# One 512-column product in place of two of 256 in the z gate of the second mixer

## The chip, the cores and the metric

The kernel runs on one core of a Trainium2 chip. The metric is device time in microseconds (us) of one execution. Before the change three runs took 1121.48, 1123.04 and 1123.1 us; the median is 1123.04 us. Lower is better.

## The reference

The program is a two-layer language-model block on 256 tokens with a width of 2048, all in float32. Layer one is an RWKV-7 mixer, layer two a sparse attention (NSA) mixer with 16 heads of 128 columns, each on a normalised input and with a residual. The part that the change touches is the gate z of the second mixer. Cut to what matters:

```python
def nsa_mixer(u, shared, w_in, gate_b, w_o):
    proj = u @ w_in                      # u: 256 tokens x 2048
    q  = rope_partial(proj[..., :2048])  # 16 heads
    gl = proj[..., 2048:2096] + gate_b   # 48 branch gates
    z  = proj[..., 2096:]                # 2048 columns: the z gate
    o  = attention(q, gl, shared)        # 256 x 2048
    o  = o * silu(z)
    return o @ w_o
```

`u` is the hidden state times the inverse root-mean-square of its token and a gain per column. The kernel multiplies by the gain before the product and by the token's factor after it.

## The kernel before

**Split numbers.** The matrix products take operands of the type float32r. Each float32 operand is split into a high part (the value copied into float32r, on ACT) and a low part (what is left, a subtraction on DVE, in some cases on POOL). A product of two operands is then three matrix products: high by high, high by low, low by high. The program calls the parts of a weight `whi` and `wlo`, those of a token tile `mh` and `ml`.

**Weights.** All weight matrices stream from HBM once, in 128x1024 pieces on the queue of SP (`Weights.load`, buffers `wraw`, five of them). A piece is split into units of 128x512 by `Weights.ensure`: line 206 is the ACT copy into `whi`, line 191 the subtraction into `wlo`. Five buffers of each exist in this stage, and a unit is taken by `W.get()`.

**Token tiles.** A mixed or normalised input is held transposed, as 16 tiles of 128 columns by 256 tokens (index k), each with a high and a low buffer. Two rings of 16 buffers serve all phases (`ring`, line 409): ring 0 holds the inputs v, k, y and ob, ring 1 holds w, a, z, r and u. `u`, the input of the second mixer, is written by `turn_h` (lines 1397 and 1398) long before it is read.

**Two forms of the product.** `rows_step` (lines 608, 609 and 611) has the tokens as the stationary operand and 512 (or 384, 432 or 256) weight columns as the moving one. `cols_step` (lines 626 to 628) has a 128x128 block of the weight as the stationary operand and 256 tokens as the moving one; its result is transposed, with columns on partitions. The z gate of the second mixer uses `cols_block`, which is four calls of `cols_step`: for each of 16 k three products of 256 columns, in the order `whi` by `mh`, `whi` by `ml`, `wlo` by `mh`, all added up in one half of a PSUM bank.

**The attention stage.** Twenty-one phases run one after the other in the order of the list `QZ` (line 80): five `phase_q`, which project the queries with `rows_step` (432, 512 or 384 columns), and 16 `phase_z`, one for each head. The list is `(0, 25, 24, 1, 2, 23, 22, 21, 3, 20, ...)`, where numbers below 10 are q and n stands for the gate of head n - 10 otherwise. Beside them a background generator, `attn_all`, computes the attention of the heads in pairs, last heads first. Its instructions have a higher rank (`atPE=1000`), and the program's scheduler, which simulates the engines in time, puts all of them into one fixed order for each engine. So the matrix products of the attention stand between those of the phases.

After its 48 products `phase_z` multiplies the sum by `RST`, the tokens' factors (line 1597, DVE, from PSUM), takes the hyperbolic tangent on ACT (line 1599) and combines both on DVE (line 1600): z times (tanh(z/2) + 1). When a pair of heads has its attention result `og` (line 1717, ACT, one buffer) and both gates, `flush` multiplies them on POOL (line 1731), splits the product (lines 1733 and 1734) and hands it to the output projection as `ob`.

**After the attention.** `phase_bo` is the output projection, with `rows_step`, from k = 15 down in its first block of 512 columns. When the last of the attention is done its buffers are released, and `open_fin` loads the residual into `h` (line 1765, 2 MB) and the final gain. `accumulate` (line 1771) adds the products to `h`. The last lines normalise and store.

**PSUM.** The products of the phases rotate over three banks (`accp("acc")`), the scores, transposes and sums of the attention have five others.

Of the kernel before, what the change touches and what calls it, by code (L numbers as in the profile page):

```python
# [11 lines left out]
F32R = mybir.dt.float32r  # L12
AF = mybir.ActivationFunctionType
OP = mybir.AluOpType
# [3 lines left out]
T, D, NK = 256, 2048, 16  # L18
# [199 lines left out]
def hybrid_kernel(ctx: ExitStack, tc: tile.TileContext, a: dict, out: bass.AP):  # L218
    nc = tc.nc
    V, S, G, PE = nc.vector, nc.scalar, nc.gpsimd, nc.tensor  # L220
# [36 lines left out]
    def accp(name="acc"):  # L257
        n = turn.get(name, 0)
        turn[name] = n + 1
        b = role[name]  # L260
        return psum.tile([128, 512], F32, name=f"bank{b[n % len(b)]}", bufs=1)
# [12 lines left out]
    W = Weights(tc, wpool, RAWB, AHEAD)  # L274
# [67 lines left out]
    mixp = ctx.enter_context(tc.tile_pool(name="mixp", bufs=1))  # L342
# [61 lines left out]

    RINGS = {"v": 0, "k": 0, "y": 0, "ob": 0, "w": 1, "a": 1, "z": 1, "r": 1, "u": 1}
    owners = ([], [])
    used = set()

    def ring(nm, k):
        i = RINGS[nm]  # L410
        h = mixp.tile([128, T], F32R, name=f"mh{i}", bufs=NK)
        l = mixp.tile([128, T], F32R, name=f"ml{i}", bufs=NK)
        owners[i].append((nm, k))
        return h, l

# [4 lines left out]
    def split_into(src, nm, k):  # L420
        h, l = ring(nm, k)
        S.activation(h, src, AF.Copy)  # L422
        V.tensor_tensor(l, src, h.bitcast(F32), op=OP.subtract)
        mixed[(nm, k)] = (h, l)
# [44 lines left out]
    if True:  # L469
# [20 lines left out]
        keep_warm(4)  # L490
        W.hold = True
        h0, l0 = ring("v", 0)
        m0 = ph1.tile([128, T], F32, name="mtmp", bufs=3)

# [100 lines left out]
    N256, N512 = 109.0, 216.0  # L595

    def need(key):
        if key not in mixed:
            sch.require(lambda: key in mixed)
        return mixed[key]  # L600
# [20 lines left out]
    def cols_step(o, nm, q, first=True, **kw):  # L621
        wh, wl = W.get()
        for s in range(4):
            k = 4 * q + s
            mh, ml = need((nm, k))
            PE.matmul(o, wh[:, s, :], mh, start=k == 0 and first, stop=False, **kw)  # L626
            PE.matmul(o, wh[:, s, :], ml, start=False, stop=False, **kw)  # L627
            PE.matmul(o, wl[:, s, :], mh, start=False, stop=k == NK - 1, **kw)  # L628
            yield 3 * N256

    def cols_block(nm, o):
        for q in range(4):
            yield from cols_step(o, nm, q)
# [42 lines left out]
    def phase_z(nb):  # L676
        ps = two()
        yield from rows_block(ps, "z", 512)
        for tt in range(2):
            th = kph.tile([128, 512], F32, name="zth", bufs=2)  # L680
            S.activation(th, ps[tt], AF.Tanh, scale=0.5)
            S.activation(th, th, AF.Copy, scale=0.5, bias=0.5)
            V.tensor_tensor(th, ps[tt], th, op=OP.mult)
            store_heads(zd, nb, tt, th, nc.sync)
# [266 lines left out]
    for nm, i in ZK:  # L951
        sch.run((phase_z3() if i == 3 else phase_z(i)) if nm == "z" else phase_k(i))
# [217 lines left out]
    def turn_y(U):  # L1170
        yt = [PBK[U][:, x * 512:x * 512 + 256] for x in range(2)]
        for i in range(NCH):
            for x, h in each:
                r = H(x, h)
                PE.matmul(yt[x][R[h], i * 64:i * 64 + 64], OU[U][r, x, i, :], ident[r, r], start=True, **mm)
        made = [ring("y", 2 * U + x) for x in range(2)]
        for x, (yh, yl) in enumerate(made):
            S.activation(yh, yt[x], AF.Copy)
            mixed[("y", 2 * U + x)] = (yh, yl)
        for x, (yh, yl) in enumerate(made):  # L1180
            V.tensor_tensor(yl, yt[x], yh.bitcast(F32), op=OP.subtract)
        sch.t += 350
# [367 lines left out]
    RST = at.tile([128, T], F32, name="RST")  # L1550
# [39 lines left out]
            qd[h0 + g] = (qh, ql)  # L1590

    def phase_z(h):
        o = accp("acc")[:, :T]
        yield from cols_block("u", o)
        sch.require(lambda: h + ZB >= HEADS or ("ob", h + ZB) in mixed)
        z = at.tile([128, T], F32, name="zT", bufs=ZB)
        V.tensor_tensor(z, o, RST, op=OP.mult)
        th = at.tile([128, T], F32, name="zth", bufs=2)
        S.activation(th, z, AF.Tanh, scale=0.5)
        V.scalar_tensor_tensor(z, th, 1.0, z, op0=OP.add, op1=OP.mult)  # L1600
        zdone[h] = z
# [147 lines left out]
    for ph in QZ:  # L1749
        sch.run(phase_q(ph) if ph < 10 else phase_z(ph - 10))  # L1750
# [95 lines left out]
```

## Time and profile before

| | us |
|---|---|
| runs | 1121.48, 1123.04, 1123.1 |
| median of the runs | 1123.04 |
| span of the profiled execution, first to last instruction | 1121.7 |
| PE busy | 1101.1 |
| DVE busy | 826.7 |
| ACT busy | 720.8 |
| POOL busy | 332.1 |
| z gates of the second mixer, first to last product | 802.6 to 1024.0 |

The profile is of one execution. Its span runs from the first to the last instruction, and the runs' median is 1.3 us longer than it. A busy PE in this profile is not a PE at its peak, since its instructions overlap: a matrix product is shown with its whole latency, and the next starts before it ends. What tells the speed of PE is the distance between the starts of two products. PEld is the loading of the stationary operand, which overlaps with the products.

### The profile page before, as it was taken

The numbers are of one execution on the slowest core, as the hardware profiler recorded it, in microseconds if no ns is written. First come the engines' busy times: TensorE is split into PE (matmuls) and PEld (weight loads), VectorE is DVE, ScalarE is ACT, GpSimd is POOL, SyncE is SP. The second block draws the span as 40 slices with busy tenths as digits, with TensorE's granted clock in tenths as the row PEclk, the third lists the DMA queues.
The fourth block names the chain that finished last, engine by engine and source line by source line (L and its number), as shares of the span: only waits on it lengthen the run. The fifth ranks groups of instructions, "written<-read, shape, count | busy, mean of one in ns | idle before, by whom it ended". The sixth has DMA issues, their size and how long they took to land.

```text
span 1121.7 us, 25742 instructions
## 1 busy us (share of the span) xinstructions
PE 1101.1 (98%) x9496; PEld 975.5 (87%) x9496; DVE 826.7 (74%) x1765; ACT 720.8 (64%) x1704; POOL 332.1 (30%) x424
## 2 busy tenths in 40 slices
PE   9999999999999989999999999999999999999997
PEld 7788899898888878989888888888989999999886
DVE  6999976679886997666667776764666877766564
ACT  7767777677774456655557766665566777765553
POOL 1300045424338657754100010101323333332012
PEclk9999999999999999999999999999999999999999
DMA  7458878777879989975578667675756355554853
GB/s 258 154 189 247 244 206 257 241 215 225 251 233 264 248 191 231 225 185 148 170 239 276 195 203 258 197 256 155 199 142 163 107 153 132 132 132 163 297 184 109
DMA packets 241775, 226.34 MB, mean 202 GB/s; under 512 B 51536, under 2 KB 193200, under 8 KB 241264
## 3 DMA queue, kind: packets, MB, share of 16 engines
q1 hardware_dynamic: 236320, 219.17, 67.3%
q0 software_dynamic: 4864, 4.92, 1.7%
q8 instruction: 75, 1.23, 0.5%
q10 hardware_dynamic: 464, 0.59, 0.1%
q14 instruction: 52, 0.43, 0.1%
HBM read 200.48 MB, written 24.15 MB: 200 GB/s over the span
## 4 chain that ended last, share of the span: by engine, by line
PE 80%; DVE 10%; DMA 4%; issue 3%; ACT 3%; SPq 0%; POOL 0%; ACTq 0%; DVEq 0%; POOLq 0%
PE bank L609 12%; PE bank L611 12%; PE bank L608 12%; PE bank L626 8%; PE bank L628 7%; PE bank L627 7%; PE bank L234 5%; DVE wlo L191 5%; ACT whi L206 2%; PE pair L611 1%; PE pair L608 1%; PE pair L609 1%; DMA wraw<-in_kv_w_dram 1%; PE bank L1192 1%; PE bank L776 1%
## 5 line engine op out<-in xcount | busy, mean ns | idle before, releaser
L191 DVE TENSOR_TENSOR wlo<-wraw,whi 128x512 fp32r<-128x512 f32 (+2 forms) x616 | 437.9, 724 | 164.9 <-ACT whi L206 161.5
L206 ACT ACTIVATE whi<-wraw 128x512 fp32r<-128x512 f32 (+2 forms) x664 | 403.0, 618 | 193.8 <-PE bank L611 68.0
L626 PE MATMUL bank<-mh,whi 128*128 128x256 f32 (+1 forms) x800 | 234.7, 293 | 0.5 <-ACT whi L206 0.5
L628 PE MATMUL bank<-mh,wlo 128*128 128x256 f32 (+1 forms) x800 | 228.2, 286 | 1.0 <-DVE wlo L191 1.0
L627 PE MATMUL bank<-ml,whi 128*128 128x256 f32 (+1 forms) x800 | 227.5, 284 | 0.0
L609 PE MATMUL bank<-wlo,mh 128*128 128x512 f32 (+3 forms) x576 | 218.1, 379 | 1.3 <-DVE wlo L191 1.2
L611 PE MATMUL bank<-whi,ml 128*128 128x512 f32 (+3 forms) x576 | 215.3, 376 | 0.0
L608 PE MATMUL bank<-whi,mh 128*128 128x512 f32 (+3 forms) x576 | 190.3, 377 | 0.6 <-ACT Vt L1490 0.3
L626 PEld LDWEIGHTS bank<-mh,whi 128*128 128x128 f32 (+1 forms) x800 | 151.4, 189 | 5.9 <-ACT whi L206 1.1
L628 PEld LDWEIGHTS bank<-mh,wlo 128*128 128x128 f32 (+1 forms) x800 | 151.3, 189 | 2.7 <-DVE wlo L191 1.4
L627 PEld LDWEIGHTS bank<-ml,whi 128*128 128x128 f32 (+1 forms) x800 | 151.7, 190 | 1.6
L609 PEld LDWEIGHTS bank<-wlo,mh 128*128 128x128 f32 x576 | 108.3, 188 | 18.6 <-DVE wlo L191 2.7
L611 PEld LDWEIGHTS bank<-whi,ml 128*128 128x128 f32 x576 | 108.3, 188 | 16.1
L608 PEld LDWEIGHTS bank<-whi,mh 128*128 128x128 f32 x576 | 107.0, 188 | 17.1 <-ACT Vt L1490 0.7
L191 POOL TENSOR_TENSOR wlo<-wraw,whi 128x512 fp32r<-128x512 f32 (+2 forms) x48 | 57.4, 1196 | 186.6 <-ACT whi L206 163.5
L609 PE MATMUL bank<-wlo,kvh 128*128 128x512 f32 x192 | 76.1, 396 | 0.0
L611 PE MATMUL bank<-whi,kvl 128*128 128x512 f32 x192 | 75.2, 392 | 0.0
L608 PE MATMUL bank<-whi,kvh 128*128 128x512 f32 x192 | 66.7, 392 | 0.4 <-ACT whi L206 0.4
L422 ACT ACTIVATE mh<-mtmp 128x256 fp32r<-128x256 f32 x95 | 37.7, 409 | 17.9 <-DVE mtmp L429 16.5
L429 DVE SCALAR_TENSOR_TENSOR mtmp<-xx,prm,xn 128x256 f32<-128x256 f32 x95 | 46.5, 501 | 0.1
L609 PEld LDWEIGHTS bank<-wlo,kvh 128*128 128x128 f32 x192 | 36.1, 188 | 7.7 <-issue 0.4
L918 POOL DMA_DIRECT2D Yb<-yvd x60 | 33.2, 558 | 31.5 <-PE pair L1106 25.7
(351 smaller groups left out, 1925.8 us busy)
## 6 DMA issues: line engine op xcount, KB each, us to landing
wraw<-in_a_w_rkvz_dram SPq DMA_DIRECT2D x128, 512.0 KB, 5.4
wraw<-in_kv_w_dram SPq DMA_DIRECT2D x48, 512.0 KB, 4.4
wraw<-in_b_w_in_dram SPq DMA_DIRECT2D x40, 512.0 KB, 4.1
wraw<-in_a_w_o_dram SPq DMA_DIRECT2D x32, 512.0 KB, 4.8
wraw<-in_b_w_o_dram SPq DMA_DIRECT2D x32, 512.0 KB, 4.4
spd<-sp SPq DMA_DIRECT2D x16, 642.0 KB, 5.5
wraw<-in_b_w_in_dram SPq DMA_DIRECT2D x24, 384.0 KB, 3.3
wraw<-in_cmp_w_dram SPq DMA_DIRECT2D x16, 512.0 KB, 4.0
```

The costliest lines, as they stand in the source:

```text
L191: eng.tensor_tensor(lv, src, hv.bitcast(F32), op=OP.subtract)
L206: self.nc.scalar.activation(hv, src, AF.Copy)
L234: return fn(*args, **kw)
L422: S.activation(h, src, AF.Copy)
L429: V.scalar_tensor_tensor(m, xx[:, k, :], mu[:, k:k + 1], xn[:, k, 1:], op0=OP.mult, op1=OP.add)
L608: PE.matmul(o, mh[:, ts], wh[:, 0, :], start=k == ends[0], stop=False)
L609: PE.matmul(o, mh[:, ts], wl[:, 0, :], start=False, stop=False)
L611: PE.matmul(o, ml[:, ts], wh[:, 0, :], start=False, stop=k == ends[1])
L626: PE.matmul(o, wh[:, s, :], mh, start=k == 0 and first, stop=False, **kw)
L627: PE.matmul(o, wh[:, s, :], ml, start=False, stop=False, **kw)
L628: PE.matmul(o, wl[:, s, :], mh, start=False, stop=k == NK - 1, **kw)
L918: eng.dma_start(Yb[U % 2][at:at + 32, x, :, 32 * q:32 * q + 32], inverse(yvd[U // 4], ((2 * U + x) % 8) * 2 + h, q))
```

## The change

Ring 1 gets one buffer of 512 columns for each k instead of two of 256: the high part in the left half, the low part in the right half. In `phase_z` the two products with the stationary operand `whi` become one with 512 moving columns, which writes the whole PSUM bank: left half high by high, right half high by low. The product with `wlo` goes on adding to the left half. At the end ACT copies the right half out of PSUM, DVE adds it to the left half and DVE multiplies by `RST` in a step of its own. Ring 0, the other phases and the order of the phases stay. The other phases that use ring 1 read the halves as before.

```diff
     def ring(nm, k):
         i = RINGS[nm]
-        h = mixp.tile([128, T], F32R, name=f"mh{i}", bufs=NK)
-        l = mixp.tile([128, T], F32R, name=f"ml{i}", bufs=NK)
+        if i:
+            both = mixp.tile([128, 2 * T], F32R, name="mhl", bufs=NK)
+            h, l = both[:, :T], both[:, T:]
+            beside[(nm, k)] = both
+        else:
+            h = mixp.tile([128, T], F32R, name="mh", bufs=NK)
+            l = mixp.tile([128, T], F32R, name="ml", bufs=NK)
         owners[i].append((nm, k))
         return h, l
...
     def phase_z(h):
-        o = accp("acc")[:, :T]
-        yield from cols_block("u", o)
+        o = accp("acc")
+        for q in range(4):
+            wh, wl = W.get()
+            for s in range(4):
+                k = 4 * q + s
+                mh, ml = need(("u", k))
+                PE.matmul(o, wh[:, s, :], beside[("u", k)], start=k == 0, stop=False)
+                PE.matmul(o[:, :T], wl[:, s, :], mh, start=False, stop=k == NK - 1)
+                yield 3 * N256
         sch.require(lambda: h + ZB >= HEADS or ("ob", h + ZB) in mixed)
         z = at.tile([128, T], F32, name="zT", bufs=ZB)
-        V.tensor_tensor(z, o, RST, op=OP.mult)
         th = at.tile([128, T], F32, name="zth", bufs=2)
+        S.activation(th, o[:, T:], AF.Copy)
+        V.tensor_tensor(z, o[:, :T], th, op=OP.add)
+        V.tensor_tensor(z, z, RST, op=OP.mult)
         S.activation(th, z, AF.Tanh, scale=0.5)
         V.scalar_tensor_tensor(z, th, 1.0, z, op0=OP.add, op1=OP.mult)
         zdone[h] = z
```

More of the change, by code (lines that the diff above doesn't have):

```diff
@@ L406, in hybrid_kernel @@
     owners = ([], [])
+    beside = {}
     used = set()
```

## The prediction, made before the change was run

> **What bounds the kernel now.** I read the page first: its busy shares, its clock and its chain of waits.
>
> ```profile
> span 1121.7 us, 25742 instructions
> ...
> PE 1101.1 (98%) x9496; PEld 975.5 (87%) x9496; DVE 826.7 (74%) x1765; ACT 720.8 (64%) x1704; POOL 332.1 (30%) x424
> ...
> PEclk9999999999999999999999999999999999999999
> ...
> PE 80%; DVE 10%; DMA 4%; issue 3%; ACT 3%; SPq 0%; POOL 0%; ACTq 0%; DVEq 0%; POOLq 0%
> ```
>
> PE holds 80% of the chain that ends last. But a share over the whole kernel says nothing about this stage, so next I took the busy time in the stage of the gates, and PE's waits from 790 to 1030 us.
>
> ```profile
> core 0: us, PE busy (x) PEld busy (x) DVE busy (x) ACT busy (x) POOL busy (x), PEclk, DMA share, GB/s
> 802.00:1025.00 223.00, 223.00 (x1561) 212.78 (x1560) 162.54 (x395) 155.30 (x440) 71.41 (x70) 1.00 0.53 142
> ```
>
> ```profile
> PE bank L609 <- DVE wlo L191: 0.4, 1, 0.4
> ```
>
> PE has work in all 223 us, at full clock (1.00), and waited once, for 0.4 us. DVE works 73% of the stage and ACT 70%, DMA 53%. Here PE alone sets the pace, and a shorter stream of products is a shorter stage. Whether a wide product makes it shorter is a question of the distance between starts, which the listing in order of time shows.
>
> **What the product costs.** First a gate as it is: 46 products of 256 columns stand in this listing from the first to the last, 45 steps.
>
> ```profile
> 802.58 0.28 PE L626 MATMUL bank<-mh,whi 128*128 128x256 f32 x1
> 802.70 0.28 PE L627 MATMUL bank<-ml,whi 128*128 128x256 f32 x1
> ...
> 807.97 0.28 PE L626 MATMUL bank<-mh,whi 128*128 128x256 f32 x1
> ```
>
> (807.97 - 802.58) / 45 = 119.8 ns. The 0.28 us of a row is latency, not the price. Then a stretch of products of 512 columns in the output projection, 16 steps.
>
> ```profile
> 1049.83 0.39 PE L608 MATMUL bank<-whi,mh 128*128 128x512 f32 x1
> 1050.05 0.39 PE L609 MATMUL bank<-wlo,mh 128*128 128x512 f32 x1
> ...
> 1053.45 0.39 PE L611 MATMUL bank<-whi,ml 128*128 128x512 f32 x1
> ```
>
> (1053.45 - 1049.83) / 16 = 226.3 ns. So 256 more columns cost 226.3 - 119.8 = 106.5 ns, and what is left of the narrow step, 119.8 - 106.5 = 13.3 ns, is paid once per product whatever its width. Two narrow ones cost 239.6 ns, one wide one 226.3: the change saves this 13.3 ns at each pair. The number of columns that stream through PE, 768 for each k, stays. This is why the saving is small: a third of the products goes, but only a fixed part of each goes with it.
>
> The number of pairs comes from the groups by shape in the stage, one such row for each of the lines 626 to 628:
>
> ```profile
> L628 PE MATMUL bank<-mh,wlo 128*128 128x256 f32 x256 | 73.4, 287 | 0.0
> L627 PE MATMUL bank<-ml,whi 128*128 128x256 f32 x256 | 73.1, 286 | 0.0
> ```
>
> 256 pairs (16 gates by 16 k) by 13.3 ns are **3.4 us less on PE**.
>
> In the new stream wide and narrow products alternate, which neither stretch shows. The nearest rows are places where one of the attention's wide products falls into a gate:
>
> ```profile
> 1020.76 0.28 PE L626 MATMUL bank<-mh,whi 128*128 128x256 f32 x1
> 1020.88 0.39 PE L234 MATMUL bank<-Th,vh 128*128 128x512 f32 x1
> 1021.11 0.28 PE L627 MATMUL bank<-ml,whi 128*128 128x256 f32 x1
> ...
> 1021.70 0.28 PE L626 MATMUL bank<-mh,whi 128*128 128x256 f32 x1
> 1021.82 0.40 PE L234 MATMUL bank<-Tl,vh 128*128 128x512 f32 x1
> 1022.06 0.27 PE L234 MATMUL bank<-cst,P 128*128 128x128 f32 x1
> ```
>
> Narrow to wide is 0.12 us and wide to narrow 0.23 (1020.88 to 1021.11), together 0.35 against three narrow steps of 0.36: some 10 ns saved. With the 0.24 of the second place, ahead of a transpose, it is 0. So the ends are 0 and 3.4 us; I take 3.3, by the first place and the pure stretches, since the second place differs in what follows.
>
> [...]
>
> **What is added.** Each gate gets one copy on ACT from PSUM and one operation on DVE. The nearest rows are an ACT copy of this shape from PSUM (line 1588), and for DVE the operations of the gate itself: 1597 reads PSUM, as the new addition will, and 1600 reads SBUF, as the new multiplication will.
>
> ```profile
> L1588 ACT ACTIVATE qh<-bank x16: 366/385/395, 808.5 to 967.8; 128x256 fp32r<-128x256 f32 x16
> ```
>
> ```profile
> L1597 DVE TENSOR_TENSOR zT<-bank,RST x16: 414/424/425, 809.0 to 1024.3; 128x256 f32<-128x256 f32 x16
> L1599 ACT ACTIVATE zth<-zT x16: 403/413/428, 809.6 to 1025.1; 128x256 f32<-128x256 f32 x16
> L1600 DVE SCALAR_TENSOR_TENSOR zT<-zth,zT x16: 380/420/1374, 810.0 to 1025.8; 128x256 f32<-128x256 f32 x16
> ```
>
> ACT gets 16 x 0.385 = 6.2 us, DVE 16 x 0.42 = 6.7 us. ACT goes from 155.3 to 161.5 of now 219.7 us (74%), DVE from 162.5 to 169.3 (77%). Both stay below PE, so I put them at 0 us. Their cover is the time in which ACT waits for PE, when it has run ahead with the weights:
>
> ```profile
> ACT whi L206 <- PE bank L611: 23.0, 41, 1.0
> ACT whi L206 <- PE bank L627: 16.4, 24, 2.0
> ACT Th L1684 <- PE bank L234: 11.0, 15, 1.9
> ```
>
> The two rows of the weights alone are 39.4 us, six times the 6.2. Without that cover the price would be up to 6.2 + 6.7 = 12.9 us.
>
> The gate also comes later after its last product: by the copy, the second DVE operation and ACT's queue, 0.8 us at least. While the copy stands at the head of ACT's queue for the last product, the splits of weights behind it wait too, and PE waits for those; but line 1597 made DVE stand there in the same way before, and five units of weights are split ahead. Two things use the gate or its bank next. The PSUM bank is needed again after at least one other gate of 48 x 0.12 = 5.8 us, so 0.8 us are free. And the attention's `og` waits on POOL:
>
> ```profile
> POOL og L1731 <- DVE zT L1600: 14.0, 6, 5.5
> ```
>
> ```profile
> 978.51 0.75 POOL L1734 TENSOR_TENSOR ml<-og,mh 128x256 fp32r<-128x256 f32 x1 [0.59 <-ACT mh L1733]
> ```
>
> ```profile
> 982.08 0.60 ACT L1717 ACTIVATE og<-bank 128x512 f32<-128x512 f32 x1 [1.08 <-PE bank L234]
> ```
>
> In 6 of 16 cases the gate is last, but at this one the buffer is free at 979.3 and refilled at 982.1, for which ACT waits on PE: 2.8 us of room. And each earlier gate has brought the stream forward by 0.2 us. I put this at 0, too.
>
> **What is only moved.** With one buffer for both halves a reader of the high part could wait for the writing of the low part, in all phases of ring 1. PE's wait for a freshly written tile is in the view of line 626:
>
> ```profile
>   ACT mh L422: 0.4, 2
> ```
>
> Two waits, 0.4 us in 800 products; waiting for the low half as well would be 0.4 us more each, 0.8 in all. I take 0, as the product that needs the low half comes 0.12 us later anyway. No DMA and no step on SP's or POOL's queue is moved.
>
> **The end of the stage.** The last pair's attention ends on POOL; then the residual is loaded, and DVE adds the first block to it.
>
> ```profile
> 1031.80 2.27 POOL L1734 TENSOR_TENSOR ml<-og,mh 128x256 fp32r<-128x256 f32 x2
> ```
>
> ```profile
> 1034.97 0.46 SPq L1765 DMA_DIRECT2D h<-hd  x1
> ```
>
> ```profile
> 1046.38 0.69 DVE L191 TENSOR_TENSOR wlo<-wraw,whi 128x512 fp32r<-128x512 f32 x1 [0.67 <-ACT whi L206]
> 1047.36 1.29 DVE L1771 TENSOR_TENSOR h<-bank,h 128x512 f32<-128x512 f32 x2 [0.28 <-DMA h<-hd]
> ```
>
> DVE already waits 0.28 us for that load. If the attention ends at the same time as now while PE's stream is 3.3 us earlier, DVE stands 3.6 us with splits of weights behind it. Four split units (4 x 6 x 0.2263 = 5.4 us of PE) less the work to catch up (1.29 + 0.69) cover 3.4, so 0.2 us reach PE. But the attention's products stand in PE's order between those of the gates and its copies wait for PE (the 11.0 us above), so most of it will move along. I take 0.
>
> **Sum:** -3.3 + 0. The profiled span of 1121.7 becomes 1118.4; the median of the runs lies 1.3 above the span, so 1123.0 becomes **1119.7 us** (-0.3%). A difference under about 0.2% (2.2 us) can't be told from none for this kernel.
>
> **Rivals.** (B) *The alternating pair costs the same.* If a wide product beside a narrow one costs 0.24 us, as at 1021.82, the pair saves nothing: 1123.0. For it: that row; against it: 0.23 at 1020.88, and 13.3 ns that both pure stretches show. [...]
>
> (C) *The scheduler's new fixed order puts a product ahead of its operand.* The order is made anew from simulated times, and the attention's products may land too early. What such a wait costs is shown earlier in the kernel:
>
> ```profile
> PE pair L1106 <- ACT X L1101: 1.7, 4, 0.7
> ```
>
> 0.43 us each; one for each of eight pairs is 3.4 us, and the gain is gone: 1123.1. Against it: the only wait of the present order in this stage is 0.4 us.
>
> (D) *Slower: the attention ends late.* If half of the 12.9 us added on ACT and DVE lengthens the attention's own chain, it ends 6.5 us later, the residual lands later, DVE stands at line 1771 and PE runs out of weights: 6.5 + 0.2 lost, 3.3 gained, 1126.4. It decides from 3.1 us of delay. For it: the load has no room (0.28). Against: the waits on PE within the chain.
>
> **Chances.** Forecast 0.60, B 0.10, C 0.14, D 0.16. The forecast's own range is 1118.4 to 1121.0, wide by the 0.8 us of the ring and the runs' 1.6 us of spread. B and C lie at 1122.4 to 1123.1; the range takes them in and the nearer part of D: 1117.8 to 1126.0. Faster 0.58 (a little of the forecast falls inside 0.2%), same 0.26, slower 0.16.
>
> **What would show it.** In the changed profile: steps of about 0.35 us for a pair within a gate; 512 products of these lines in place of 768; the gates some 3 us shorter from first to last product; PE's waits in the stage still near 0.4 us; DVE's wait ahead of line 1771 under 3.6 us. Wrong would be pair steps of 0.36 (B), new waits of PE for `Th`, `Tl` or `P` (C), or weights missing after line 1771 (D).

## The result, and the profile after

The changed kernel takes 1132.38 us (median of four runs, 1132.06 to 1133.25) against 1123.07 us before (also of four runs; the three of the prediction gave 1123.04). The ratio is 1.0084, with a 95% interval of 1.007 to 1.0098: slower by 9.3 us. The forecast was 1119.7 us.

The page of the profile after, its span, busy times, clock and chain:

```profile
span 1130.7 us, 25249 instructions
...
PE 1101.2 (97%) x9240; PEld 962.9 (85%) x9240; DVE 833.1 (74%) x1781; ACT 726.0 (64%) x1720; POOL 332.4 (29%) x424
...
PEclk9999999999999999999999999999999999999899
...
PE 85%; DVE 7%; issue 2%; ACT 2%; DMA 2%; POOL 1%; SPq 0%; ACTq 0%; DVEq 0%; POOLq 0%
```

256 products are gone (9496 to 9240), and the busy time of PE has not changed. One digit of the clock is new: an 8 near the end of the span. PE's share of the chain has even risen, from 80% to 85%, and tells nothing. The view that does is that of PE's waits; its two largest rows are new:

```profile
PE bank L614 <- DVE h L1786: 6.0, 1, 6.0
PE bank L614 <- ACT mh L1748: 2.0, 1, 2.0
```

Line 614 is the first product of `rows_step` (608 before), line 1786 the addition of the residual (1771 before), line 1748 the high part of the attention's `ob` (1733 before). Both waits are single ones, and both lie after the gates.

**In the gates the change did what it says.** PE's listing in order of time, from the first product of the first gate to that of its 17th pair, and then the last gate product of the stage:

```profile
803.60 0.40 PE L1605 MATMUL bank<-mhl,whi 128*128 128x512 f32 x1
803.83 0.28 PE L1606 MATMUL bank<-mhl,wlo 128*128 128x256 f32 x1
...
809.23 0.40 PE L1605 MATMUL bank<-mhl,whi 128*128 128x512 f32 x1
...
1017.62 0.28 PE L1606 MATMUL bank<-mhl,wlo 128*128 128x256 f32 x1
```

(809.23 - 803.60) / 16 = 351.9 ns for a wide and a narrow product, against 3 x 119.8 = 359.4 ns before. Over all the steps of this form in the stage's listing (212 after, 206 before) the means are 354 and 362 ns, again 7.5 ns less. For 256 pairs that is 1.9 us in all. The gates end at 1017.62, not at 1023.99:

```profile
1023.99 0.28 PE L628 MATMUL bank<-mh,wlo 128*128 128x256 f32 x1
```

They end 6.4 us earlier while PE saved only 1.9 us. So other work that stood between the gates before now stands behind them. It is the attention's. Its last product for a pair of heads has the operands `Th` and `vcs`; the view of that tile, first before and then after:

```profile
L234 PE MATMUL bank<-Th,vcs x8: 393/394/483, 848.8 to 1029.1; 128*128 128x512 f32 x8
```

```profile
L234 PE MATMUL bank<-Th,vcs x8: 389/393/398, 850.1 to 1043.1; 128*128 128x512 f32 x8
```

The first pair of heads is 1.3 us late (the stage starts 1.0 us later in this execution, 803.60 against 802.58), the eighth 14.0 us. The period of a pair has gone from (1029.1 - 848.8) / 7 = 25.8 us to 27.6 us. PE has no wait of 0.2 us or more in this stretch: the attention's products are not waiting for anything, they stand later in PE's fixed order. What stands ahead of them is shown by the groups of PE between the last gate product and the last attention product, after (1017.7 to 1043.0) and before (1024.2 to 1029.0):

```profile
L615 PE MATMUL bank<-wlo,mh 128*128 128x512 f32 x28 | 11.0, 395 | 0.0
L617 PE MATMUL bank<-whi,ml 128*128 128x512 f32 x28 | 11.0, 393 | 0.0
L614 PE MATMUL bank<-whi,mh 128*128 128x512 f32 x28 | 10.6, 394 | 0.0
```

```profile
L608 PE MATMUL bank<-whi,mh 128*128 128x512 f32 x7 | 2.7, 391 | 0.0
L611 PE MATMUL bank<-whi,ml 128*128 128x512 f32 x6 | 2.3, 390 | 0.0
L609 PE MATMUL bank<-wlo,mh 128*128 128x512 f32 x6 | 2.3, 390 | 0.0
```

84 products of the output projection in place of 19. The 65 more are 65 x 0.2263 = 14.7 us of PE. And 84 is everything in the first block that does without the last pair of heads: 14 of its 16 k, six products each. What stands next in PE's order, behind the last attention product, needs that pair.

**What the late attention costs.** The attention's last step on POOL, the issue of the residual's load on SP's queue behind it, and the first addition on DVE, each from the listing after (the rows of before stand in the prediction):

```profile
1045.67 1.44 POOL L1749 TENSOR_TENSOR ml<-og,mh 128x256 fp32r<-128x256 f32 x2
```

```profile
1047.53 0.89 SPq L1780 DMA_DIRECT2D h<-hd  x1
```

```profile
1057.24 1.29 DVE L1786 TENSOR_TENSOR h<-bank,h 128x512 f32<-128x512 f32 x2 [6.84 <-DMA h<-hd]
```

POOL ends at 1047.1, before at 1034.1: 13.0 us late. The load is issued 12.6 us late, and DVE stands 6.84 us for it, before 0.28. The load does not take the same time in both: from issue to landing the view of the DMA issues has 12.3 us before and 9.6 us after, so 2.7 us of the delay come back there.

A PSUM bank of the first block is not free until the addition has been made, so PE stops, for 6.03 us. PE's listing at that place:

```profile
1043.14 0.40 PE L234 MATMUL bank<-Th,vcs 128*128 128x512 f32 x1
1045.53 0.50 PE L614 MATMUL bank<-whi,mh 128*128 128x512 f32 x1 [2.00 <-ACT mh L1748]
...
1051.56 0.39 PE L617 MATMUL bank<-whi,ml 128*128 128x512 f32 x1
1057.98 0.79 PE L614 MATMUL bank<-whi,mh 128*128 128x512 f32 x1 [6.03 <-DVE h L1786]
1058.58 0.63 PE L615 MATMUL bank<-wlo,mh 128*128 128x512 f32 x1
...
1061.99 0.42 PE L614 MATMUL bank<-whi,mh 128*128 128x512 f32 x1
```

With 0.23 us as the usual step, the two gaps are 2.39 - 0.23 = 2.2 us and 6.42 - 0.23 = 6.2 us. Then nine steps take 4.01 us where 9 x 0.2263 = 2.0 us is usual: 2.0 us more, at a granted clock of 0.50 (1058 to 1062 us). The busy times from 1000 to 1100 show the same three losses, PE 92 us of 100 and a clock of 0.97, before 99.55 and 1.00:

```profile
1000.00:1100.00 100.00, 91.97 (x440) 76.39 (x439) 60.22 (x107) 54.23 (x119) 14.41 (x16) 0.97 0.53 183
```

```profile
1000.00:1100.00 100.00, 99.55 (x562) 87.13 (x561) 64.39 (x103) 57.85 (x120) 18.57 (x19) 1.00 0.60 200
```

The account: 1.0 (later start) + 2.2 + 6.2 + 2.0 - 1.9 = 9.5 us, against 1130.7 - 1121.7 = 9.0 us between the spans.

### The profile page after: what moved, and what is told of

It reads as the page before. It is cut to its first block, busy times and chain, and to the rows that moved or that the text cites. A ratio compares the mean times of both kernels' runs of the same rounds, so it can differ in the third digit from the quotient of the medians.

```text
span 1130.7 us, 25249 instructions
## 1 busy us (share of the span) xinstructions
PE 1101.2 (97%) x9240; PEld 962.9 (85%) x9240; DVE 833.1 (74%) x1781; ACT 726.0 (64%) x1720; POOL 332.4 (29%) x424
## 4 chain that ended last, share of the span: by engine, by line
PE 85%; DVE 7%; issue 2%; ACT 2%; DMA 2%; POOL 1%; SPq 0%; ACTq 0%; DVEq 0%; POOLq 0%
PE bank L615 13%; PE bank L614 13%; PE bank L617 13%; PE bank L632 6%; PE bank L1605 5%; PE bank L634 5%; PE bank L633 5%; PE bank L234 5%; DVE wlo L191 3%; PE bank L1606 3%; PE pair L617 1%; PE pair L614 1%; PE pair L615 1%; PE pair L1118 1%; PE bank L1198 1%
## 5 line engine op out<-in xcount | busy, mean ns | idle before, releaser
L615 PE MATMUL bank<-wlo,mh 128*128 128x512 f32 (+1 forms) x288 | 110.3, 384 | 0.8 <-DVE wlo L191 0.7
L617 PE MATMUL bank<-whi,ml 128*128 128x512 f32 (+1 forms) x288 | 108.2, 381 | 0.0
L615 PE MATMUL bank<-wlo,mhl 128*128 128x512 f32 (+2 forms) x288 | 108.1, 375 | 0.0
L617 PE MATMUL bank<-whi,mhl 128*128 128x512 f32 (+2 forms) x288 | 107.7, 374 | 0.0
L614 PE MATMUL bank<-whi,mh 128*128 128x512 f32 (+1 forms) x288 | 94.5, 384 | 8.3 <-DVE h L1786 6.0
L614 PE MATMUL bank<-whi,mhl 128*128 128x512 f32 (+2 forms) x288 | 99.1, 374 | 0.3 <-ACT Vt L1496 0.3
L1605 PE MATMUL bank<-mhl,whi 128*128 128x512 f32 x256 | 92.7, 399 | 0.0
L632 PE MATMUL bank<-mhl,whi 128*128 128x256 f32 (+1 forms) x288 | 87.7, 304 | 0.0
L634 PE MATMUL bank<-mhl,wlo 128*128 128x256 f32 (+1 forms) x288 | 82.1, 285 | 1.0 <-DVE wlo L191 1.0
L633 PE MATMUL bank<-mhl,whi 128*128 128x256 f32 (+1 forms) x288 | 82.1, 285 | 0.0
L632 PE MATMUL bank<-mh,whi 128*128 128x256 f32 x256 | 74.8, 292 | 0.4 <-ACT whi L206 0.4
L634 PE MATMUL bank<-mh,wlo 128*128 128x256 f32 x256 | 73.4, 288 | 0.0
```

The lines of the kernel that those rows point to most:

```text
L614: PE.matmul(o, mh[:, ts], wh[:, 0, :], start=k == ends[0], stop=False)
L615: PE.matmul(o, mh[:, ts], wl[:, 0, :], start=False, stop=False)
L617: PE.matmul(o, ml[:, ts], wh[:, 0, :], start=False, stop=k == ends[1])
L1605: PE.matmul(o, wh[:, s, :], beside[("u", k)], start=k == 0, stop=False)
```

## The experiments

Three theories stood at the start; the expectations call them O, L and R. *Order*: the wide products make the scheduler put the attention later in PE's order. *Length*: the 12.9 us of new work on ACT and DVE lengthen the attention's own chain (that was the cause that rival D named). *Ring*: the joint buffer costs something. Each part of the change was first run without the others, except that the joint buffer stays in the first two runs; the third has it alone. The edits are shown against the changed kernel, except where the text names the kernel before. All ratios are to the kernel before, with a 95% interval.

**The wide product without the new end.**

```diff
-        S.activation(th, o[:, T:], AF.Copy)
-        V.tensor_tensor(z, o[:, :T], th, op=OP.add)
-        V.tensor_tensor(z, z, RST, op=OP.mult)
+        V.tensor_tensor(z, o[:, :T], RST, op=OP.mult)
```

> The changed kernel with the wide product, but with the gate's end of before: line 1597's product with RST on the left half alone. The right half (u low by weight high) is computed and left out of the result, so ACT and DVE have the work of before (12.9 us less than in the changed kernel). Theory L (the added work on ACT and DVE lengthens the attention): the attention ends at about 1034 us of the span as before, PE keeps the 2.4 us of its shorter pairs, 1120.7 us. Theory O (with the wide product the scheduler's simulated clock runs the gates faster beside the attention, so it puts the attention's products later into PE's fixed order, whatever the ends of the gates cost): the attention still ends at 1044 to 1048, DVE still waits for the residual at the first addition, 1130 to 1133.5 us. Theory R (the joint buffer): slow as well, 1130 to 1133.5.

The right half of the bank is computed here and left out of the result. Measured 1130.79 us, ratio 1.0082 (1.0063 to 1.01). PE's waits have the same two rows:

```profile
PE bank L614 <- DVE h L1784: 4.1, 1, 4.1
PE bank L614 <- ACT mh L1746: 2.0, 1, 2.0
```

The last attention product starts at 1041.85 (after 1043.14). So nearly all of the loss comes with the wide product, without any added work on ACT or DVE.

**The new end and the joint buffer, with three narrow products.**

```diff
-                PE.matmul(o, wh[:, s, :], beside[("u", k)], start=k == 0, stop=False)
+                PE.matmul(o[:, :T], wh[:, s, :], mh, start=k == 0, stop=False)
+                PE.matmul(o[:, T:], wh[:, s, :], ml, start=False, stop=False, skip_group_check=True)
```

> The changed kernel with three narrow products (two into the left half, u low into the right half) and with the changed end of the gate: ACT copy, addition, product with RST. Joint buffers stay. Theory L: the attention is late by up to 13 us and the 2.4 us of the pairs are lost too, 1132 to 1135 us. Theory O: PE's order is that of before, the added work hides under PE, attention's end at 1033 to 1037, 1122.5 to 1124.5 us. Theory R: slow, 1131 to 1135.

Measured 1122.76 us, ratio 1.0001 (0.999 to 1.0012). The added work is there, and costs nothing that can be measured. The attention does end later, POOL at 1034.76 + 2.35 = 1037.1, which is 3.0 us late, but DVE's wait has grown by only 0.33 us and PE has no wait:

```profile
1034.76 2.35 POOL L1750 TENSOR_TENSOR ml<-og,mh 128x256 fp32r<-128x256 f32 x2
```

```profile
1049.36 1.29 DVE L1787 TENSOR_TENSOR h<-bank,h 128x512 f32<-128x512 f32 x2 [0.61 <-DMA h<-hd]
```

**The joint buffer alone**, with `phase_z` as before:

```diff
     def phase_z(h):
-        o = accp("acc")
...
+        o = accp("acc")[:, :T]
+        yield from cols_block("u", o)
```

> The kernel before with nothing but the joint buffers of ring 1: narrow products and the old end of the gate. Theories L and O: nothing depends on it, 1122.3 to 1123.9 us. Theory R: most of the loss, 1130 or more.

Measured 1123.23 us, ratio 1.001 (0.9997 to 1.0022). The ring costs nothing that can be measured; POOL ends at 1034.4, where it did before. *Length* and *Ring* have fallen as causes of the 9.3 us.

**How the delay grows with the number of wide gates.** The changed kernel with wide products in the last eight gates only (heads 0 to 7, as in the diff), then in the last four (`range(0, 4)`); the others have two narrow products into the two halves, and the new end stays everywhere.

```diff
-                PE.matmul(o, wh[:, s, :], beside[("u", k)], start=k == 0, stop=False)
+                if h in range(0, 8):
+                    PE.matmul(o, wh[:, s, :], beside[("u", k)], start=k == 0, stop=False)
+                else:
+                    PE.matmul(o[:, :T], wh[:, s, :], mh, start=k == 0, stop=False)
+                    PE.matmul(o[:, T:], wh[:, s, :], ml, start=False, stop=False, skip_group_check=True)
```

> The changed kernel with the wide product in the last eight gates alone (heads 7 to 0); the first eight gates have three narrow products, two into the left half and one into the right. Theory O, by the order of the program: between the last gate's product and the attention's last one stand 64 products of the output projection (19 before, 84 in the changed kernel), so the attention ends at about 1043 us of the span; the waits for the residual stay, that for ob nearly goes: 1127 to 1131 us, less the half of the pairs' gain. If the loss came all at once with the first wide products or with the joint end of the gates, it would be as slow as the changed kernel, 1132.

> The same with the wide product in the last four gates alone (heads 3 to 0): 39 products between, attention's end at about 1038 us, no wait for ob, some 2 to 4 us for the residual at the first addition: 1123.5 to 1127 us. With no wait at all it would be 1122.

Measured 1128.11 us, ratio 1.0041 (1.0023 to 1.006), with eight, and 1123.2 us, ratio 0.9997 (0.9986 to 1.0007), with four. PE's one wait of the run with eight:

```profile
PE bank L614 <- DVE h L1790: 4.4, 1, 4.4
```

With four there is none, and DVE does not wait for the residual:

```profile
1049.32 1.29 DVE L1790 TENSOR_TENSOR h<-bank,h 128x512 f32<-128x512 f32 x2
```

| wide gates | first gate product | end of the attention on POOL | late by | late by, from the first gate product | PE's wait for the addition |
|---|---|---|---|---|---|
| 0 (new end only) | 804.1 | 1037.1 | 3.0 | 1.5 | 0 |
| 4 | 803.7 | 1039.5 | 5.5 | 4.3 | 0 |
| 8 | 801.8 | 1042.8 | 8.7 | 9.5 | 4.4 |
| 16 | 803.6 | 1047.1 | 13.0 | 12.0 | 6.0, and 2.0 for `mh` |

The executions do not begin the stage at the same time (802.6 before), so the column that counts from the first gate product is the one to compare. From 0 to 4, 8 and 16 wide gates the delay grows by 2.8, 8.0 and 10.5 us, that is by 0.7, 1.0 and 0.7 us for each. PE saves only 16 x 7.5 ns = 0.12 us in a gate. And the loss has a threshold: it begins somewhere between 4.3 and 9.5 us of delay. The prediction had it at 3.1, and the expectation of the run with four wide gates had a wait of 2 to 4 us for the residual, which did not come. The prediction counted with a load of unchanged length. In the run with four gates it was issued at 1039.96 and had landed by 1049.32, in at most 9.4 us. Against the 12.3 us of before that gives back at least 2.9 of the 5.0 us by which it was issued late.

**The end of the stage without its load.** The changed kernel, with the first 512 columns of the residual loaded ahead of the attention; one of three buffers of `Th` and `Tl` makes room for them.

```diff
+    h20 = early.tile([128, 2, 512], F32, name="h20")
+    nc.sync.dma_start(h20, hd[:, 0:512].rearrange("(a p) c -> p a c", p=128))
...
-        nc.sync.dma_start(h2, hd.rearrange("(a p) c -> p a c", p=128))
+        nc.sync.dma_start(h2[:, :, 512:], hd[:, 512:].rearrange("(a p) c -> p a c", p=128))
...
-        V.tensor_tensor(hv, ps, hv, op=OP.add)
+        V.tensor_tensor(hv, ps, h20[:, tt, :] if i == 0 else hv, op=OP.add)
```

> The changed kernel with the first 512 columns of the residual (512 KB) loaded into a buffer of their own before the attention begins, so that the first addition of line 1771 doesn't wait for a load that starts at the attention's end; one buffer less of Th and Tl (2 instead of 3) makes room. If the late residual is what turns the attention's delay into time: PE's stall of 6.0 us and the 2.0 us at a lower clock behind it go, the 2.0 us of waiting for ob stay, 1123.5 to 1125.5 us. If the wait only moves to the residual of the next blocks or to the weights: 1129 us or more.

Measured 1123.99 us, ratio 1.0015 (1.0006 to 1.0025); the same edit in the kernel before gives 1121.76 us, ratio 0.9991 (0.9979 to 1.0002):

> The control of the early residual: the kernel before the change with the first 512 columns of the residual loaded ahead of the attention and with one buffer less of Th and Tl. No wait to speak of goes (0.28 us at line 1771), so 1122 to 1123.5 us.

In the changed kernel the edit takes back most of the loss; by the medians it stays 2.2 us above its control. The attention still ends late, POOL at 1044.2, but DVE adds at 1046.08 without waiting for the residual, and of PE's two waits one is left:

```profile
PE bank L614 <- ACT mh L1751: 2.0, 1, 2.0
```

The profiled execution of this run took 1121.3 us, 2.7 less than the run's median, at a granted clock of 0.999. Of the ten executions two have this clock, at 1120.67 and 1121.3 us; the other eight have 0.994 to 0.997 and took 1122.88 to 1125.97 us. That fits a stretch of slow clock behind the 2.0 us of waiting (last section), but no trace of one of the eight exists, so it is not shown.

**Lateness without wide products.** The kernel before, with only the order of the phases changed, so that the query phases 1 and 2 come later and the attention with them.

```diff
-QZ = (0, 25, 24, 1, 2, 23, 22, 21, 3, 20, 19, 18, 4, 17, 16, 15, 14, 13, 12, 11, 10)
+QZ = (0, 25, 24, 23, 22, 21, 1, 2, 3, 20, 19, 18, 4, 17, 16, 15, 14, 13, 12, 11, 10)
```

> The kernel before, narrow products, separate buffers and old gate end, with only the list of phases changed: the second block of queries comes after the gates 23, 22 and 21 instead of ahead of them, so that the attention of heads 9 to 12 can't begin until then and its last products come late in PE's order, as in the changed kernel. Theory O (what costs time is the attention's place in the order, not the wide product): attention's end at 1043 to 1050 us of the span, PE waits 6 to 10 us for ob and for the residual's addition, 1129 to 1135 us. If lateness alone costs nothing: 1122 to 1124.

Measured 1141.03 us, ratio 1.016 (1.0145 to 1.0175): slower than any theory said. The attention ends at 1058.5 on POOL, 24.5 us late. The waits of PE:

```profile
PE bank L608 <- DVE h L1771: 5.6, 1, 5.6
PE bank L234 <- DVE P L1660: 2.2, 1, 2.2
PE bank L608 <- ACT mh L1733: 2.0, 1, 2.0
PE bank L234 <- DVE ql L1589: 0.9, 1, 0.9
```

The first and the third are the pair of the changed kernel, at nearly the same sizes, without one wide gate product. The other two lie inside the stage, between 913 and 923 us, where before PE was busy throughout at a clock of 1.00:

```profile
900.00:1000.00 100.00, 96.61 (x677) 91.90 (x676) 75.24 (x183) 70.85 (x211) 33.60 (x33) 0.95 0.46 119
```

3.4 us of PE are idle here, and the clock of 0.95 takes more; no theory had counted on that. So this run shows that a late attention makes the two waits at the end, but its total is not a price of the lateness alone. Nor do the two waits grow with the lateness: they are no longer at 24.5 us than at 13.0.

**Work to put in the gap.** If PE only stands because nothing is left that does without the last `ob` and the residual, other work at that place should take all of it back. The block of 256 columns from 1536 of the output projection is computed, but for its own last two k, ahead of the last two k of the first block, into the third bank (`po`; `quarter` takes two k of this block), and the blocks behind use four other banks.

```diff
+        po = accp()
+        for k in range(NK - 1, 1, -1):
+            yield from rows_step(ps, "ob", k, W.get(), 512, (NK - 1, 0))
+        for m in range(7, 0, -1):
+            yield from quarter(m)
+        for k in (1, 0):
+            yield from rows_step(ps, "ob", k, W.get(), 512, (NK - 1, 0))
+        yield from quarter(0)
+        open_fin()
...
-        banks(acc=(2, 3, 0, 1))
+        banks(acc=(4, 5, 6, 7))
```

> The changed kernel with another order at the start of the output projection: the block of 256 columns from 1536 is computed between k = 2 and k = 1 of the first block, in the third PSUM bank of the phases, so that PE has 10 us more of products that need no more of the attention than k = 15 to 2; the later blocks use banks 4 to 7. The attention may end as late as in the changed kernel (1047). Theory O: the two waits at the end (2.0 and 6.0 us) and the slow clock behind them go, what is left is the 2.4 us that the pairs save: 1119.5 to 1121 us. If the wide product costs something else as well: 1123 or more.

> The control of the run before: the same order of the output projection in the kernel before the change. There the attention ends at 1034 and nothing waits for it, so 1122 to 1123.5 us. If it is faster by more than 1 us, the new order has a merit of its own.

Measured 1119.59 us, ratio 0.9968 (0.9957 to 0.998), in the changed kernel, and 1121.55 us, ratio 0.9996 (0.9983 to 1.0009), in the kernel before. The attention is as late as in the changed kernel (its last product starts at 1043.07), and DVE still waits for the load, but PE has work in all 100 us at a clock of 1.00:

```profile
1060.27 1.95 DVE L1791 TENSOR_TENSOR h<-bank,h 128x512 f32<-128x512 f32 x4 [1.69 <-DMA h<-hd]
```

```profile
1000.00:1100.00 100.00, 100.00 (x531) 85.73 (x530) 68.78 (x119) 58.15 (x127) 16.82 (x17) 1.00 0.55 192
```

With the gap covered the wide product brings 1121.55 - 1119.59 = 2.0 us by the medians and 3.1 us by the two ratios. Their intervals do not overlap, so the sign is clear; the size agrees roughly with what the pair steps said (1.9; the 2.4 us of the expectations was the author's estimate). The changed kernel in this version is faster than both kernels. The control lies 1.4 us below its own runs of the kernel before by the medians and 0.4 us by the ratio, whose interval holds 1; a merit of the new order by itself is not shown. The run does two things at once: the added work fills PE's time, and with four other banks the next block needn't wait for the addition. The first is what covers the wait for `mh`, as PE's listing has those 256-column products at 1043.31, right behind the last attention product. Which of the two removes the second wait is not separated. The delay by itself need not cost anything; what stands at the end of the stage turns it into a loss.

## Why the prediction was wrong

**What bounds the kernel** was read rightly, and still holds: PE sets the pace in the gates, and no wait of 0.2 us or more came up inside the stage: after, PE has work in all 200 us from 800 to 1000, at a clock of 1.00.

**The pair** was mis-sized, with the right sign: 13.3 ns forecast, as a part that a product pays whatever its width, and 7.5 measured for the pair, so 1.9 us in place of 3.4 (3.3 taken). The nearest row, 0.12 + 0.23 at 1020.88, gave some 10 ns and was nearer than the pure stretches, which went into the sum. The listing of the alternating stream has 0.23 and 0.12, as that row has. Rival B, no gain at all, is refuted by the pair steps and by the sign of the last experiment. The forecast's range lets B and C begin at 1122.4, and no run shows that figure: B by its own row stands at 1123.0, and with the 7.5 ns that were measured the pairs alone would give 1123.0 - 1.9 = 1121.1.

**What is added** was right at nothing. The copy and the two DVE operations cost what the rows of before said (view by line, after; the second DVE operation, line 1613, has a median of 426 ns):

```profile
L1611 ACT ACTIVATE zth<-bank x16: 365/367/380, 809.9 to 1018.4; 128x256 f32<-128x256 f32 x16
```

```profile
L1612 DVE TENSOR_TENSOR zT<-bank,zth x16: 411/418/425, 810.3 to 1019.1; 128x256 f32<-128x256 f32 x16
```

The run with the new end alone is at 1.0001. **What is only moved**, the ring, was right at nothing too (1.001, its interval holds 1).

**The end of the stage** is the step that failed. It said that DVE's load has no room, that 3.4 us would be covered, and then: "But the attention's products stand in PE's order between those of the gates and its copies wait for PE (the 11.0 us above), so most of it will move along. I take 0." It took PE's order as given, with the products in it nearer together. The order is made anew for each kernel. In the new one the attention's products come behind 65 more products of the output projection, and the attention ends 13.0 us later while the gates end 6.4 us earlier.

**Rival C** said that the order is made anew and let it err on the other side, products too early for their operands. There was no such wait.

**Rival D** had the place, the load, the standing DVE and the sign. Its cause was wrong: not half of 12.9 us of added work, but the order. Counted from the first gate product, the run with the new end alone is 1.5 us late on POOL and loses nothing; the run with the wide product and no added work is 12.0 us late, as late as the changed kernel. That the 13.0 us of delay nearly equal the 12.9 us of added work is chance. What PE waited for was not as D had it either: it did not run out of weights (no wait for `wlo` or `whi` stands in PE's waits from 1000 us on), it waited for a bank that the addition had to empty. D's price of 6.5 + 0.2 for 6.5 us of delay was wrong as well. The delay begins to count somewhere between 4.3 and 9.5 us, not from 3.1, and then it costs more than D counted: two gaps of PE (2.2 and 6.2 us), and a clock of 0.50 behind the second.

**What stays open.** Why the scheduler puts the attention later is argued, not shown. It places products by a clock of its own, on which a gate may get shorter by more than the 0.12 us that PE saves. The 0.7 to 1.0 us of delay for a gate and these 0.12 are 0.8 to 1.1 us, or some 50 to 70 ns for a pair, which its clock would have to save to give the order that is seen. The pace that the kernel itself sets is not it: `yield 3 * N256` charges each k the same in both kernels. What the scheduler charges for a product was not measured. The wide product also lowers the number of instructions, and no run separates that from what they are charged. That the wide products change the order is shown by the runs with 0, 4, 8 and 16 wide gates.

## What to carry to other kernels

Where a planner sets a fixed order, a cheaper instruction is not only a shorter one: the order around it is made anew, so look for what shares the engine, and ask what ends last if it comes later. Then look at the end of the stage: how many microseconds of delay can the first consumer of a late load bear, and what work is there to put in its place? Here a gain of 2 us was lost to two gaps of 8 us together. It came back when a block of independent work was moved there and the blocks behind it got other banks.

## What the runs showed of the hardware that was not expected

**Some gaps of PE were paid for longer than they lasted.** Behind the gap of 6.2 us in the changed kernel the step of a 512-column product was (1061.56 - 1059.00) / 6 = 0.43 us in place of 0.2263, for 4.0 us, at a granted clock of 0.50 (1058 to 1062 us; 0.99 from 1062 to 1063):

```profile
1059.00 0.63 PE L617 MATMUL bank<-whi,ml 128*128 128x512 f32 x1
...
1061.56 0.61 PE L617 MATMUL bank<-whi,ml 128*128 128x512 f32 x1
```

In the run with the wide product and the old end the short gap ahead of line 614 did the same:

```profile
1041.85 0.40 PE L234 MATMUL bank<-Th,vcs 128*128 128x512 f32 x1
1044.24 0.79 PE L614 MATMUL bank<-whi,mh 128*128 128x512 f32 x1 [2.00 <-ACT mh L1746]
1044.83 0.63 PE L615 MATMUL bank<-wlo,mh 128*128 128x512 f32 x1
1045.26 0.63 PE L614 MATMUL bank<-whi,mh 128*128 128x512 f32 x1
...
1047.74 0.40 PE L614 MATMUL bank<-whi,mh 128*128 128x512 f32 x1
```

For 3.5 us behind a gap of 2.2 us the steps are slow (0.43 from 1044.83 on). In the changed kernel a gap of the same 2.2 us, at 1045.53, had no such tail: the next product came 0.34 us later (1045.87), and the one behind it 0.23 us after that. The gaps for `mh` in the run with the early residual and in the run with the other order of phases had no tail either: behind the first the steps are 0.34 and 0.23 us, and from 1000 to 1060 us, with the second in it, the clock is 1.00. But the latter run's gap inside the stage, 2.3 us with PE busy before it, has one, and from 900 to 925 us the clock is 0.82:

```profile
916.04 0.76 PE L234 MATMUL bank<-kh,qh 128*128 128x512 f32 x1 [2.18 <-DVE P L1660]
916.60 0.63 PE L234 MATMUL bank<-kl,qh 128*128 128x512 f32 x1
917.02 0.63 PE L234 MATMUL bank<-kh,ql 128*128 128x512 f32 x1
```

So two of five gaps of this size were followed by slow steps. Behind the longer gaps of the runs with eight wide gates and with the old end (4.4 and 4.1 us of waiting) the slow steps lasted about 3 and 5 us. The slow step is 1.9 times the usual one (0.43 against 0.2263 us), and slow steps went on for 3 to 5 us where the listing shows their end. How long a gap must be for this is not shown: gaps of about 2.2 us did it twice and three times not. In these runs such a gap cost its 2.2 us alone or nearly 4, with 3.50 - 8 x 0.2263 = 1.7 us behind it in the run with the wide product and the old end.
